# Three matmul passes over split operands in place of f32 matmuls, for the output projection and the memory attention's projections of the last four tiles

## The chip, the cores and the metric

The kernel runs on one core of one Trainium2 chip. The metric is the device time of one execution in microseconds (us), given as the median of several runs. The core has five engines that work side by side, each through its own instruction stream in order: TensorE (PE) multiplies matrices, VectorE (DVE) and ScalarE (ACT) do elementwise work and reductions, GpSimd (POOL) does elementwise work too, and SyncE (SP) issues most of the DMAs. Matmuls read SBUF and write PSUM.

## The reference

One transformer layer over 1024 tokens of width 1024, in f32: a mixer of two sparse attentions, then cross attention to a memory of 256 tokens, then an MLP with a squared ReLU.

```python
x = x + _hybrid_mixer(_rms_norm(x, norm1_g[l]), ...)      # ends with: return o @ w_out
x = x + _memory_xattn(_rms_norm(x, norm2_g[l]), mem, ...)
x = x + _sq_relu_mlp(_rms_norm(x, norm3_g[l]), w_ff_in[l], w_ff_out[l])

def _memory_xattn(h, mem, mem_norm_g, w_xq, w_xk, w_xv, xq_norm_g, xk_norm_g, w_xo):
    q = _rms_norm((h @ w_xq).reshape(B, L, XATTN_HEADS, XATTN_HEAD_DIM), xq_norm_g)
    ...
    p = jax.nn.softmax(s, axis=-1).astype(v.dtype)
    ...
    return o @ w_xo
```

The change bears on three of these products for tokens 512 to 1023: `o @ w_out` (1024 by 1024), `h @ w_xq` (1024 by 512) and `o @ w_xo` (512 by 1024).

## The kernel before

The tokens are eight tiles of 128. The kernel first projects tiles 0 to 3 (`project`, part 0). Then `together` interleaves two generators: the attention of all tiles (`attend`), and a filler, `fill`, that projects the other half, prepares the memory's keys and values, and then runs `between` on tiles 0 and 1, `between` on tiles 2 and 3, `mlp` on tiles 0 to 3, and `between` on tiles 4 and 5. Each step of a generator yields an estimate of its TensorE time, and the filler goes on while its sum is below the attention's sum times a pace (`PACES`). When attention is through, its buffers are given up, the pool `d2` is opened in their place, and `merge` interleaves what is left of the filler with `between` on tiles 6 and 7, in the ratio 70 to 45. Last comes `mlp` on tiles 4 to 7. This order of the program is the priority that a scheduler then uses: it places the instructions of every engine by a simulated timeline, and puts the waits in.

`between` (L894) does, for its `nt` = 2 tiles: load the attention's output `o` from DRAM (eight transfers a tile, L900) and the residual `x`; the product with `w_out` in four chunks of 256 columns, added to `x` by `residual_add` (L891) on VectorE; the second norm (`norm_T2`, L290), which squares the tile into the buffer of the transposed activations and then has TensorE transpose it in groups of four blocks (`to_T`, L268); the product with `w_xq` in two chunks, each followed by attention over the memory (`memory_item`), whose result goes to DRAM (`xo_dr`); this result comes back, is transposed, and is multiplied by `w_xo` in four chunks. There are two streams of it here: tiles 4 and 5 in the pool `dn`, tiles 6 and 7 in the pool `d2`.

`gemm` (L300) is the one function for these products. It takes the activations as a list `xs`. With one entry they are f32: a piece of the weights of 256 rows by 256 columns is fetched by `load_whole` (L261) into a buffer of the rings `whi` and `wlo` by turns, and each block of 128 rows, 128 tokens and 256 columns is one f32 matmul, which appears in the trace as two instructions. With two entries they are a rounded part and a remainder in the type fp32r: `load_w` (L251) fetches the same piece into a buffer of the ring `wraw`, `split_w` (L240) copies it to `whi` (rounded) on one engine and writes the remainder to `wlo` on another, and each block is three matmuls: high by high, high by low, low by high. The engines of `split_w` follow a plan of letter pairs, the first for the copy, the second for the remainder (a: ScalarE, v: VectorE, g: GpSimd): `PLAN_MAIN` is "ag", `PLAN_TAIL` (L46) "ag", "av", "ag" by turns. Before, `between` always calls `gemm` with one entry; `mlp` and the first part of `project` use two. `split_ps` (L234) splits activations: a ScalarE copy and a VectorE subtraction. `to_T` uses it where two outputs are asked for; for one output it copies once, with ScalarE for the first group.

The rings have these depths: in `dn` `wraw` 2, `whi` 4, `wlo` 4; in `d2` `wraw` 3, `whi` 6, `wlo` 6. `xT` (L328) gives the buffers of transposed activations, `xh` and for two entries `xl`; each exists once in a pool, so a second call waits until the first one's readers are done. The MLP at the end uses the same rings and `xh`, `xl` of `d2`.

Of the kernel before, what the change touches and what calls it, by code (L numbers as in the profile page):

```python
# [22 lines left out]
P = 128  # L23
# [22 lines left out]
PLAN_TAIL = ("ag", "av", "ag")  # L46
# [34 lines left out]
REST = 70.0  # L81


def drain(gen):
    for _ in gen:
        pass


def beside(ga, ta, gb, tb):

    da = db = 0.0
    la = lb = True
    while la or lb:
        if la and (not lb or da * tb <= db * ta):
            w = next(ga, None)
            la = w is not None
            da += w or 0.0
        else:
            w = next(gb, None)
            lb = w is not None  # L100
            db += w or 0.0
        if w is not None:
            yield w


def merge(a, b):
    drain(beside(*a, *b))
# [59 lines left out]
def build(nc, tc, I, C, out):  # L167
    v, s, g, te = nc.vector, nc.scalar, nc.gpsimd, nc.tensor
    ctx = ExitStack()
    W = {n: I[n][0] for n in I}  # L170
# [63 lines left out]
    def split_ps(src, hi, lo):  # L234
        s.activation(hi, src, AF.Copy)  # L235
        v.tensor_tensor(lo, src, hi, op=ALU.subtract)  # L236

    plan = {"i": 0, "w": PLAN_MAIN}
# [12 lines left out]
    def load_w(pool, shape, *srcs):  # L251
        raw = ring(pool, "wraw", shape)
        for dst, src in srcs:
            nc.sync.dma_start(dst(raw), src)
        hi, lo = ring(pool, "whi", shape, F32R), ring(pool, "wlo", shape, F32R)
        split_w(raw, hi, lo)
        return hi, lo
# [3 lines left out]
    def load_whole(pool, shape, *srcs):  # L261
        wholes["i"] += 1
        raw = ring(pool, ("whi", "wlo")[wholes["i"] % 2], shape)
        for dst, src in srcs:
            nc.sync.dma_start(dst(raw), src)
        return [raw]
# [33 lines left out]
    def gemm(pool, xs, nk, nt, wsrc, chunks, consume):  # L300

        for ci, parts in enumerate(chunks):
            w = sum(n for _, n in parts)
            gr = []
            for k0 in range(0, nk, KG):
                kn = min(KG, nk - k0)
                srcs, o = [], 0
                for c0, n in parts:
                    srcs.append((lambda r, o=o, n=n: r[:, :, o:o + n],
                                 wsrc[k0 * P:(k0 + kn) * P, c0:c0 + n].rearrange("(k p) n -> p k n", p=P)))  # L310
                    o += n
                ws = load_w(pool, [P, kn, w], *srcs) if len(xs) == 2 else load_whole(pool, [P, kn, w], *srcs)
                gr += [[x[:, k, :] for x in ws] for k in range(kn)]
            for t in range(nt):
                pt = pst(TAGS[pool.name][0], [P, w])
                for k in range(nk):
                    if len(xs) == 1:
                        mm(pt, xs[0](t, k), gr[k][0], k == 0, k == nk - 1)
                        continue
                    wh, wl = gr[k]  # L320
                    xh, xl = xs[0](t, k), xs[1](t, k)
                    mm(pt, xh, wh, k == 0, False)
                    mm(pt, xh, wl, False, False)
                    mm(pt, xl, wh, False, k == nk - 1)
                consume(ci, t, pt)
                yield nk * (5 - len(xs)) * w / 2400.0

    def xT(pool, nt, whole=False):  # L328

        parts = [pool.tile([P, DM // P, nt * P], F32 if whole else F32R, tag="x" + n, name="x" + n)  # L330
                 for n in ("h" if whole else "hl")]
        return (parts, [lambda t, k, x=x: x[:, k, t * P:(t + 1) * P] for x in parts],
                lambda t: [x[:, :, t * P:(t + 1) * P] for x in parts])
# [557 lines left out]
            v.tensor_tensor(dst, pt, dst, op=ALU.add)  # L891
        return add_to

    def between(pool, t0, nt, x2s, keep):  # L894

        o_of = []
        for t in range(nt):
# [6 lines left out]
            nc.sync.dma_start(x2[t], I["x"][0, (t0 + t) * P:(t0 + t + 1) * P, :])  # L904
        add_to = residual_add(x2)
        four = [[(c * 256, 256)] for c in range(4)]
        yield from gemm(pool, [lambda t, k: o_of[t][:, k, :]], 8, nt, W["w_out"], four, add_to)
        _, xf, xt_of = xT(pool, nt, True)

        gb2 = gain2(pool, W["norm2_g"])  # L910
        for t in range(nt):
# [179 lines left out]
    def fill():  # L1091
        for part in range(1, len(PARTS)):
            with tc.tile_pool(name="p2", bufs=1, reuse_waits="tile") as p2:
                yield from project(p2, part, pe, st)
            projected.append(part)
        dn = dn_pool.__enter__()
        yield from memory(dn)
        yield 1, PACES[1]
        yield from between(dn, 0, 2, {}, False)
        yield 3, PACES[2]  # L1100
        x2s = {}
        yield from between(dn, 2, 2, x2s, True)
        yield 3, PACES[3]
        yield from mlp(dn, 0, 4, x2s)
        yield 5, PACES[4]
        yield from between(dn, 4, 2, {}, False)

    rest = fill()
    together(attend(aw, st), rest, projected)
# [4 lines left out]
    d2 = d2_pool.__enter__()  # L1114
    x2s = {}
    rest = (w for w in rest if not isinstance(w, tuple))
    merge((rest, REST), (between(d2, 6, 2, x2s, True), 45.0))
    dn_pool.__exit__(None, None, None)
    drain(mlp(d2, 4, 4, x2s))
    d2_pool.__exit__(None, None, None)  # L1120
# [22 lines left out]
```

## Time and profile before

| | |
|---|---|
| median of 3 runs | 1814.33 us (1814.0 to 1814.47) |
| profiled execution | 1807.76 us |
| its span, first to last instruction | 1806.0 us |
| TensorE busy | 1700.2 us, 94% |
| ScalarE, VectorE, GpSimd busy | 1061.9, 927.8, 887.4 us |
| HBM traffic | 185.38 MB by DMA, 103 GB/s on the mean |
| mean granted TensorE clock | 0.976 |

Rows of the profile name engine, line, operation and buffers as out<-in, with a count and a mean time. Buffers have the names of the kernel's tags: `psD`, `psS`, `psM`, `psPT` are PSUM; `b` holds residuals and the attention's output; `xh`, `xl` are activations, `whi`, `wlo`, `wraw` weights. In stream 4 and 5 the products go to `psD`, in stream 6 and 7 to `psS`. Matmuls are pipelined: a row's mean time is longer than the distance from one start to the next, so rates are taken from starts and counts.

### The profile page before, as it was taken

Reading aid. Unit: us, or ns where it says so; the run is one execution under the profiler, and the core shown is the slowest. Engines: PE = TensorE matmul, PEld = TensorE weight load, DVE = VectorE, ACT = ScalarE, POOL = GpSimd, SP = SyncE. Lnnn points to the kernel's source line nnn. Section 1 sums busy time; section 2 is a strip of 40 time slices with the busy share of each in tenths; the row PEclk is TensorE's granted clock in tenths of the full one; section 3 lists DMA queues with packets and bytes.
Section 4 is the critical chain, followed back from the end, with each engine's and each line's share of the span. In section 5 each row is a group of like instructions: output and inputs, shape, how many; then the busy total and the mean of one; then the engine's idle time right before and its main releaser. Section 6 shows DMA issues by size and latency. Waiting matters only on the chain. (4 is left out here: it accounts for less than half of the span.)

```text
span 1806.0 us, 27690 instructions
## 1 busy us (share of the span) xinstructions
PE 1700.2 (94%) x9134; PEld 1447.8 (80%) x9134; DVE 927.8 (51%) x2343; ACT 1061.9 (59%) x2655; POOL 887.4 (49%) x1015
## 2 busy tenths in 40 slices
PE   5987999899989999999998999999999799999998
PEld 5986888688878777788886888888888687787887
DVE  4545757665874776375754555646524322222221
ACT  4445669797688579855896558994513333333332
POOL 2356647363541355568575667662111144545444
PEclk9998999999999999999999999999999799999999
DMA  6235221366336211212122212226384122222222
GB/s 193 73 121 155 70 68 58 114 196 175 102 109 196 87 59 42 75 65 80 59 75 75 62 65 78 65 74 194 98 284 151 47 87 89 97 91 96 94 95 93
DMA packets 171887, 185.38 MB, mean 103 GB/s; under 512 B 26464, under 2 KB 140896, under 8 KB 171744
## 3 DMA queue, kind: packets, MB, share of 16 engines
q1 hardware_dynamic: 163808, 173.13, 30.3%
q0 software_dynamic: 7936, 10.49, 2.2%
q8 instruction: 72, 1.18, 0.3%
q14 instruction: 71, 0.58, 0.1%
HBM read 162.59 MB, written 20.97 MB: 102 GB/s over the span
## 5 line engine op out<-in xcount | busy, mean ns | idle before, releaser
L249 POOL TENSOR_TENSOR wlo<-wraw,whi 128x512 fp32r<-128x512 f32 (+1 forms) x231 | 310.6, 1351 | 280.9 <-ACT whi L244 252.9
L244 ACT ACTIVATE whi<-wraw 128x512 fp32r<-128x512 f32 (+2 forms) x289 | 181.0, 628 | 250.8 <-PE psS L218 156.8
L218 PE MATMUL psD<-whi,xh 128*128 128x256 f32 (+1 forms) x704 | 191.1, 352 | 4.4 <-ACT whi L244 3.4
L218 PE MATMUL psD<-wlo,xh 128*128 128x256 f32 (+1 forms) x704 | 190.3, 352 | 1.6 <-DMA wlo<-in_w_in_dram 1.0
L236 DVE TENSOR_TENSOR pl<-psPT,ph 128x512 fp32r<-128x512 f32 (+1 forms) x232 | 142.1, 621 | 78.9 <-ACT ph L235 76.3
L218 PE MATMUL psD<-whi,h 128*128 128x512 f32 x512 | 174.3, 403 | 3.7 <-ACT whi L244 1.6
L218 PE MATMUL psS<-whi,h 128*128 128x512 f32 x512 | 162.4, 392 | 5.4 <-DVE b L891 5.4
L680 ACT ACTIVATE S<-S,mn 128x128 f32<-128x128 f32 (+7 forms) x192 | 142.7, 744 | 40.5 <-DVE mn L678 39.0
L685 POOL TENSOR_SCALAR S<-S,sums,gi 128x640 f32<-128x640 f32 (+7 forms) x128 | 107.8, 853 | 114.1 <-DVE sums L683 103.5
L235 ACT ACTIVATE ph<-psPT 128x512 fp32r<-128x512 f32 (+1 forms) x232 | 122.9, 540 | 61.5 <-PE psPT L695 57.1
L249 DVE TENSOR_TENSOR wlo<-wraw,whi 128x512 fp32r<-128x512 f32 (+1 forms) x58 | 56.3, 971 | 170.3 <-ACT whi L244 170.1
L218 PEld LDWEIGHTS psD<-wlo,xh 128*128 128x128 f32 x704 | 132.4, 193 | 13.6 <-DMA wlo<-in_w_in_dram 1.4
L218 PEld LDWEIGHTS psD<-whi,xh 128*128 128x128 f32 x704 | 130.0, 193 | 14.2 <-ACT whi L244 3.8
L695 PE MATMUL psPT<-c_ident,S 128*128 128x128 f32 x816 | 131.8, 277 | 3.9 <-POOL S L685 2.6
L891 DVE TENSOR_TENSOR b<-psS,b 128x512 f32<-128x512 f32 (+1 forms) x80 | 49.9, 636 | 138.5 <-PE psS L218 138.5
L218 PE MATMUL psS<-K,qh 128*128 128x384 f32 (+3 forms) x288 | 112.4, 394 | 8.9 <-DVE mn L678 3.9
L218 PEld LDWEIGHTS psS<-whi,h 128*128 128x128 f32 x512 | 96.0, 188 | 30.4 <-DVE b L891 10.1
L218 PEld LDWEIGHTS psD<-whi,h 128*128 128x128 f32 x512 | 95.5, 189 | 25.8 <-ACT whi L244 2.0
L695 PEld LDWEIGHTS psPT<-c_ident,S 128*128 128x128 f32 x816 | 97.6, 142 | 14.1 <-POOL S L685 4.5
L218 PE MATMUL psD<-wlo,h 128*128 128x512 f32 x256 | 102.6, 404 | 1.1 <-POOL wlo L249 1.1
L218 PE MATMUL psD<-xh,wlo 128*128 128x512 f32 x256 | 101.5, 398 | 0.0
L891 DVE TENSOR_TENSOR b<-psD,b 128x512 f32<-128x512 f32 (+1 forms) x112 | 63.2, 573 | 74.0 <-PE psD L218 66.9
(289 smaller groups left out, 4546.2 us busy)
## 6 DMA issues: line engine op xcount, KB each, us to landing
wraw<-in_w_ff_in_dram SPq DMA_DIRECT2D x128, 256.0 KB, 2.7
wraw<-in_w_ff_out_dram SPq DMA_DIRECT2D x128, 256.0 KB, 2.6
whi<-in_w_out_dram SPq DMA_DIRECT2D x32, 256.0 KB, 3.8
wlo<-in_w_out_dram SPq DMA_DIRECT2D x32, 256.0 KB, 4.3
wraw<-in_w_in_dram SPq DMA_DIRECT2D x24, 256.0 KB, 3.4
q<-st SPq DMA_DIRECT2D x12, 512.0 KB, 2.6
qin<-q SPq DMA_DIRECT2D x44, 128.0 KB, 2.3
x<-in_x_dram SPq DMA_DIRECT2D x8, 512.0 KB, 5.5
```

What stands on the lines that cost most here:

```text
L218: te.matmul(o, a, b, start=start, stop=stop)
L235: s.activation(hi, src, AF.Copy)
L236: v.tensor_tensor(lo, src, hi, op=ALU.subtract)
L244: s.activation(hi, raw, AF.Copy)
L249: (v if l == "v" else g).tensor_tensor(lo, raw, hi, op=ALU.subtract)
L680: s.activation(S, S, AF.Exp, bias=low, scale=-1.0, accum_out=sums[:, hh:hh + 1])
L685: g.tensor_scalar(Ss[hh], Ss[hh], sums[:, hh:hh + 1], 1.0 if gate is None else gate[:, hh:hh + 1], op0=ALU.mult, op1=ALU.mult)
L695: te.transpose(p2[:, j, hh, :], S[:, (c + j) * P:(c + j + 1) * P], ident)
L891: v.tensor_tensor(dst, pt, dst, op=ALU.add)
```

## The change

For tiles 4 to 7, `between` gets `whole=False`. The attention's output is split into a rounded part and a remainder, the transposed activations of `w_xq` and `w_xo` are written as two parts, and the weights of all three products are split as they arrive. `PLAN_TAIL` holds from `between` on tiles 4 and 5 on, where before it began at the opening of `d2`. Tiles 0 to 3 stay as they are.

```diff
-    def between(pool, t0, nt, x2s, keep):
+    def between(pool, t0, nt, x2s, keep, whole):
...
         four = [[(c * 256, 256)] for c in range(4)]
-        yield from gemm(pool, [lambda t, k: o_of[t][:, k, :]], 8, nt, W["w_out"], four, add_to)
-        _, xf, xt_of = xT(pool, nt, True)
+        if whole:
+            xf = [lambda t, k: o_of[t][:, k, :]]
+        else:
+            parts, xf, _ = xT(pool, nt)
+            for t in range(nt):
+                ts_ = slice(t * P, (t + 1) * P)
+                for c in range(0, 8, 4):
+                    split_ps(o_of[t][:, c:c + 4, :], *[x[:, c:c + 4, ts_] for x in parts])
+        yield from gemm(pool, xf, 8, nt, W["w_out"], four, add_to)
+        _, xf, xt_of = xT(pool, nt, whole)
...
-        yield from between(dn, 0, 2, {}, False)
+        yield from between(dn, 0, 2, {}, False, True)
...
-        yield from between(dn, 2, 2, x2s, True)
+        yield from between(dn, 2, 2, x2s, True, True)
...
-        yield from between(dn, 4, 2, {}, False)
+        plan["w"] = PLAN_TAIL
+        yield from between(dn, 4, 2, {}, False, False)
...
-    merge((rest, REST), (between(d2, 6, 2, x2s, True), 45.0))
+    merge((rest, REST), (between(d2, 6, 2, x2s, True, False), 45.0))
```

## The prediction

> **What bounds the kernel now.** I read the page first: its sums and its slices.
>
> ```profile
> span 1806.0 us, 27690 instructions
> PE 1700.2 (94%) x9134; PEld 1447.8 (80%) x9134; DVE 927.8 (51%) x2343; ACT 1061.9 (59%) x2655; POOL 887.4 (49%) x1015
> PE   5987999899989999999998999999999799999998
> ```
>
> TensorE is busy 94% of the span; the slices show two soft places, the beginning and slice 31 (45 us a slice, so about 1400 to 1445 us). The profiled execution took 1807.76 us, its span 1806.0; the median of the runs is 1814.33, 0.4% above. I sum changes against the trace and subtract them from the median.
>
> Next I cut out the stretch that the change touches, by windows. I call the work on tiles 4 and 5 stream A (pool dn) and that on tiles 6 and 7 stream B (pool d2).
>
> ```profile
> core 0: us, PE busy (x) PEld busy (x) DVE busy (x) ACT busy (x) POOL busy (x), PEclk, DMA share, GB/s
> 1060.00:1200.00 140.00, 139.84 (x751) 118.69 (x750) 78.11 (x191) 117.08 (x262) 95.09 (x94) 1.00 0.21 68
> 1234.00:1305.00 71.00, 69.88 (x418) 62.51 (x416) 39.95 (x102) 33.33 (x64) 17.53 (x20) 0.98 0.47 147
> 1305.00:1322.00 17.00, 15.04 (x61) 12.98 (x61) 3.41 (x9) 3.19 (x10) 4.32 (x8) 0.70 0.87 256
> 1322.00:1394.00 72.00, 70.92 (x385) 62.79 (x383) 25.61 (x71) 17.15 (x43) 8.25 (x13) 1.00 0.66 211
> 1394.00:1440.00 46.00, 34.42 (x151) 27.56 (x151) 20.28 (x46) 16.18 (x34) 6.43 (x8) 0.75 0.21 63
> 1400.00:1410.00 10.00, 6.17 (x29) 5.76 (x28) 2.23 (x4) 0.60 (x2) 0.00 (x0) 0.51 0.25 79
> ```
>
> The columns are the stretch, its length, busy time and instructions of TensorE, of its weight loads, VectorE, ScalarE and GpSimd, then TensorE's granted clock, DMA share and GB/s. The reader is to see three kinds of stage. From 1234 to 1305 stream A runs beside the attention of the last tile: TensorE is full (69.88 of 71 us). From 1322 to 1394 B and the rest of A are interleaved: full again (70.92 of 72), the other engines a quarter to a third busy or less. From 1305 to 1322 and from 1394 to 1440 chains of short steps leave it idle, and its clock falls (0.70 and 0.75). So a shorter matmul pays in the first and third stage, and only partly in the others.
>
> Then the ends of the chains, in the timelines of SyncE's DMA queue (SPq) and of TensorE (start, us, what).
>
> ```profile
> 1234.24 0.38 SPq L265 DMA_DIRECT2D whi<-in_w_out_dram  x1
> 1367.05 0.37 SPq L265 DMA_DIRECT2D wlo<-in_w_xo_dram  x1
> 1305.84 8.17 SPq L900 DMA_DIRECT2D b<-o  x16
> 1323.86 1.97 PE L218 MATMUL psS<-whi,b 128*128 128x256 f32 x8 [0.49 <-DMA whi<-in_w_out_dram]
> 1392.58 1.03 PE L218 MATMUL psS<-wlo,xh 128*128 128x256 f32 x4
> 1409.43 1.09 PE L274 MATMUL psPT<-c_ident,relu 128*128 128x128 f32 x4 [3.60 <-DMA relu<-xo]
> 1411.81 1.92 PE L218 MATMUL psS<-whi,xh 128*128 128x256 f32 x4
> 1425.79 1.03 PE L218 MATMUL psS<-wlo,xh 128*128 128x256 f32 x4
> 1439.90 0.78 PE L218 MATMUL psS<-xh,whi 128*128 128x512 f32 x1
> ```
>
> A's weights are fetched from 1234.24 to 1367.05. Attention ends at about 1305; SyncE then issues B's 16 loads of attention output, and B's first `w_out` matmul waits for its weights until 1323.86. B's `w_xq` ends at 1393, its last attention item and a trip through DRAM end at 1409.43, its `w_xo` runs from 1411.81 to 1426.6, and after the norm of four tiles the MLP begins at 1439.90. From there on the kernel is the same in both versions, so the question is when that first MLP matmul starts.
>
> **The change on TensorE.** Which products lie in which stage, by groups of instructions in the four windows; below them two rows of TensorE's timeline, and a window of the head with one of its groups:
>
> ```profile
> L218 PE MATMUL psD<-whi,b 128*128 128x256 f32 x64 | 17.0, 379 | 0.0
> L218 PE MATMUL psD<-whi,xh 128*128 128x256 f32 x16 | 4.1, 379 | 0.0
> L218 PE MATMUL psD<-whi,xh 128*128 128x256 f32 x16 | 5.4, 469 | 0.0
> L218 PE MATMUL psS<-whi,b 128*128 128x256 f32 x64 | 16.8, 382 | 0.9 <-DMA whi<-in_w_out_dram 0.5 <-DVE b L891 0.4
> L218 PE MATMUL psS<-whi,xh 128*128 128x256 f32 x32 | 8.4, 386 | 0.0
> L218 PE MATMUL psD<-whi,xh 128*128 128x256 f32 x32 | 8.3, 382 | 0.0
> L218 PE MATMUL psS<-whi,xh 128*128 128x256 f32 x32 | 9.1, 411 | 0.0
> 1416.29 1.03 PE L218 MATMUL psS<-whi,xh 128*128 128x256 f32 x4
> 1418.02 1.03 PE L218 MATMUL psS<-whi,xh 128*128 128x256 f32 x4
> 80.80:90.80 10.00, 10.00 (x90) 10.00 (x90) 2.05 (x6) 3.08 (x10) 0.99 (x1) 1.00 0.35 105
> L218 PE MATMUL psD<-wlo,xh 128*128 128x256 f32 x30 | 8.2, 276 | 0.0
> ```
>
> Each group has a twin with `wlo`, because whole weights alternate between the two rings, so 64 means 128 instructions. A 128x128x256 product in f32 is two of them. In order: A's `w_out` 64 products and half of `w_xq`, 16 (first stage); the other 16 (second); B's `w_out` 64, B's `w_xq` 32, A's `w_xo` 32 (third); B's `w_xo` 32 (last): 256. In the timeline eight f32 instructions (a row of `whi`, one of `wlo`) start within 1.73 us, so one takes 0.216 and a product 0.432 us. The three-pass price comes from the head, which does the same shapes in three passes with TensorE full: 90 matmuls touch 10 us, and at 276 ns each some 2.5 of them hang over an edge, so 10/87.5 = 0.114 us each and 0.342 a product. Each product saves 0.090 us: 80 in the first stage 7.2, 16 in the second 1.4, 128 in the third 11.5, 32 in the last 2.9, together 23.0 us of TensorE.
>
> **What it adds elsewhere.** The 64 weight loads stay, of the same size, but go through `wraw`. Each now needs a ScalarE copy and a subtraction, by the plan of the tail two in three on GpSimd. The attention output of four tiles is split too (8 copies, 8 subtractions), and 12 transposed groups get a VectorE subtraction.
>
> ```profile
> L244 ACT ACTIVATE whi<-wraw 128x512 fp32r<-128x512 f32 (+2 forms) x289 | 181.0, 628 | 250.8 <-PE psS L218 156.8
> L249 POOL TENSOR_TENSOR wlo<-wraw,whi 128x512 fp32r<-128x512 f32 (+1 forms) x231 | 310.6, 1351 | 280.9 <-ACT whi L244 252.9
> L249 DVE TENSOR_TENSOR wlo<-wraw,whi x58: 609/694/1770, 23.6 to 1780.1; 128x512 fp32r<-128x512 f32 x56, 128x448 fp32r<-128x448 f32 x2
> L236 DVE TENSOR_TENSOR pl<-psPT,ph 128x512 fp32r<-128x512 f32 x59 | 40.3, 687 | 24.6 <-ACT ph L235 23.1 <-PE psD L218 1.4
> ```
>
> ScalarE 72 x 0.63 = 45 us, GpSimd 43 x 1.35 = 58, VectorE (21 + 8 + 12) x 0.69 = 28, over 206 us in which the four windows give ScalarE 70 us, GpSimd 37, VectorE 89. All three stay below 60% busy. That such a mix holds is shown from 1060 to 1200, where the first MLP runs three passes from this same pool beside attention, with ScalarE 117 and GpSimd 95 of 140 us busy and TensorE at 139.84. I take nothing for throughput. VectorE's longest subtraction is 1.08 us over the median; the four that split B's attention output could add 4.3 us, or 0; I take 0, since VectorE idles 46 of 72 us in the third stage. The Trainium skill, "SBUF — State Buffer", section "Who interferes with whom", says that a VectorE instruction with two SBUF inputs and a GpSimd one that reads SBUF shut each other out for a whole instruction; the spread of 694 to 1770 ns agrees with that, and by the rule the time would be up to 1805 us.
>
> **What waits instead.** A whole weight could be fetched 8 (A) or 12 (B) buffers ahead. A split one occupies `wraw` (2 in dn, 3 in d2) until its subtraction is done. The turn of a `wraw` buffer in dn now, from the timelines of SyncE's queue and GpSimd, and the landing of `w_out`'s loads (least, median, most):
>
> ```profile
> 1163.97 7.59 SPq L254 DMA_DIRECT2D wraw<-in_w_ff_in_dram  x4
> 1168.17 1.31 POOL L249 TENSOR_TENSOR wlo<-wraw,whi 128x512 fp32r<-128x512 f32 x1 [1.94 <-ACT whi L244]
> DMA to landing us min/median/max: 2.6/3.9/9.0
> ```
>
> Four loads begin within 7.59 us through two buffers; the first subtraction ends at 1169.48, so a turn is 5.5 us: 2.75 us per weight tile in dn, and with three buffers 1.83 in d2. A's first 24 tiles take 66 us at that pace, as long as the stage. A cannot run ahead there, and its saved TensorE time must go to attention. Bounds: 0 (attention is held by its own chain) and 7.2; I take 4, the middle. In all A has room: 31 tile steps in 133 us, 4.3 each. Behind a split that waits for its DMA stand, on ScalarE, attention's exponentials, on GpSimd the powers of the norms and the `KX`/`VX` loads, on SyncE attention's stores and the `xo` trips; the 1060 to 1200 window has these queues in the same position, the `xo` trip excepted.
>
> Second stage: the first B tile lands when it does now and then needs 0.63 + 1.35 us. TensorE has only `w_xq` before that, so its 1.4 us are lost and 2.0 are added. Bounds -1.4 (A has other work left) and 2.0 + 1.7. The 1.7 stands for the clock: the gap would be 1.4 + 0.49 + 2.0 = 3.9 us, and after the 3.60 us wait at 1409 the clock over 1400 to 1410 was 0.51. I take +2.0.
>
> Third stage: B's `w_out` at ring pace is 16 x 1.83 = 29 us, while TensorE needs 64 x 0.342 = 22 for it; now it ends 30.5 us after its start. A's last attention item and `w_xo` (11 us) fill the difference, since A has its own ring. Split transposes add 4 x 0.69 before B's `w_xq`, beside A's work. Bounds -11.5 (all paid) and -2 (the ring sets B's pace, below); I take -10. Last stage: `w_xo` saves 2.9, two subtractions on the way cost 1.4; its 8 tiles are fetched and split in the idle stretch before (6 buffers), else one turn, 5.5 us, would show. Bounds -2.9 and +4; I take -1.5. The MLP's first raw weights, now behind `w_xo` in the same ring, have the 13 us of the norm as cover.
>
> Sum: -4 + 2 - 10 - 1.5 = -13.5 us, so 1814.3 - 13.5 = 1801 us.
>
> **The rivals.** *All of it is paid*: attention takes the whole 7.2 and filler is always at hand, -23 + 2 = -21 us: 1793. For it, TensorE full in both long stages; against it, the ring pace in the first. *Ring pace instead of TensorE pace*: a weight tile feeds four products, 1.83/4 = 0.46 us each in d2, no better than the 0.432 of f32. If B's chain alone sets the end, `w_out` gains nothing anywhere; only `w_xq` and `w_xo` of B do, 64 x 0.090 = 5.8, less 2.0 and less 1.4 at the transposes: -2 to -3, 1812. Against it, A's 18 us of work in the same stretch. *Slower, by late weights in d2*: landings of `w_out` reach 9.0 us. At a landing of 7 a turn is 9, 3.0 a tile, 48 us for B's `w_out` against 30.5: +17.5, less 4 from the first stage and 5.8, plus 2: about +10, 1824. It decides above a turn of 7.2 us (2.4 a tile). For it, DMA share 0.87 from 1305 to 1322; against it, that burst comes from deep rings, which the small ring cuts off. That the change does not do what it says I can exclude from the head, where the same function makes three-pass matmuls at 0.114 us.
>
> **How the numbers follow.** Forecast (1795 to 1807) 0.42; all paid (1789 to 1795) 0.2; ring pace (1807 to 1816) 0.16; late weights (1816 to 1835) 0.22. A change of 0.2%, 3.6 us, is about what this measurement can tell. Faster: 0.42 + 0.2 + 0.06 of ring pace = 0.68; the same 0.1; slower 0.22. The range drops the best edge and half of the late-weights case: 1790 to 1820.
>
> **What would show it.** In the changed trace: three matmuls of 128x256 at 0.114 us per product in these stages; wraw turns near 5.5 us; TensorE still full in the two long stages, with attention's end 0 to 7 us earlier; the first MLP matmul some 13 us before 1439.9 on the same clock, and the MLP after it unchanged at about 366 us. I am wrong if TensorE waits for `wlo` or `whi` for more than some 5 us in all, or if the first MLP matmul comes later.

## The result, and the profile after

The changed kernel is slower: 1822.1 us median against 1812.09 us for the kernel before on the same chip, a ratio of 1.0049 with a 95% interval of [1.0032, 1.0065], taken over all runs (the two medians alone divide to 1.0055). The forecast was 1801 us, faster. The profiled execution took 1817.73 us. Its page, the sums and the slices:

```profile
span 1816.0 us, 28472 instructions
PE 1692.0 (93%) x9390; PEld 1453.2 (80%) x9390; DVE 963.3 (53%) x2385; ACT 1102.9 (61%) x2727; POOL 942.2 (52%) x1057
PE   5987999799989999999998999998898799999999
```

TensorE's busy sum fell by 8.2 us, and the span grew by 10.0. The windows that the prediction showed of before, now of after (same columns, the last one to the later end):

```profile
1234.00:1305.00 71.00, 62.89 (x465) 57.77 (x466) 52.33 (x113) 43.24 (x81) 31.79 (x31) 0.98 0.41 126
1305.00:1322.00 17.00, 12.82 (x71) 10.80 (x69) 10.31 (x25) 8.48 (x20) 6.79 (x11) 0.75 0.70 212
1322.00:1394.00 72.00, 63.22 (x485) 61.19 (x485) 37.40 (x81) 36.44 (x73) 37.96 (x33) 0.92 0.59 190
1394.00:1453.00 59.00, 45.46 (x256) 39.82 (x256) 27.27 (x59) 22.28 (x44) 15.91 (x16) 0.72 0.37 115
```

In the first stage TensorE had 69.88 us of work before and has 62.89 now: the 7 us are there, and most of them are idle time. In the third stage it had 70.92 of 72 us and now 63.22, at a granted clock of 0.92 instead of 1.00, and the stage lasts longer. The milestones of B follow from the timeline of TensorE (start, us, what); first those of before that the prediction did not show, the last matmul of the first MLP, the end of `w_out` (the last of the four in its row starts at 1354.34) and the starts of the two chunks of `w_xq`:

```profile
1228.28 0.39 PE L218 MATMUL psD<-whi,h 128*128 128x512 f32 x1
...
1353.69 1.03 PE L218 MATMUL psS<-wlo,b 128*128 128x256 f32 x4
...
1358.44 1.08 PE L218 MATMUL psS<-whi,xh 128*128 128x256 f32 x4
...
1386.49 1.08 PE L218 MATMUL psS<-whi,xh 128*128 128x256 f32 x4
```

and those of after:

```profile
1230.75 0.40 PE L218 MATMUL psD<-whi,h 128*128 128x512 f32 x1
...
1323.46 0.80 PE L218 MATMUL psS<-whi,xh 128*128 128x256 f32 x2 [1.07 <-ACT whi L244]
...
1360.03 0.28 PE L218 MATMUL psS<-whi,xl 128*128 128x256 f32 x1
...
1365.12 1.11 PE L274 MATMUL psPT<-c_ident,relu 128*128 128x128 f32 x4 [3.45 <-DVE relu L297]
...
1368.24 0.56 PE L218 MATMUL psS<-whi,xh 128*128 128x256 f32 x1
...
1396.43 0.52 PE L218 MATMUL psS<-whi,xh 128*128 128x256 f32 x1
...
1425.46 0.56 PE L218 MATMUL psS<-whi,xh 128*128 128x256 f32 x1
...
1452.79 0.78 PE L218 MATMUL psS<-xh,whi 128*128 128x512 f32 x1
```

They are, in order, the last matmul of the first MLP, B's first `w_out` matmul, its last one, the first transpose of B's norm (after a wait of 3.45 us), and the first matmuls of the two `w_xq` chunks, of `w_xo` and of the last MLP. From them, and the last store of the attention (1305.15 and 1305.46, shown below):

| step (us) | before | after | difference | forecast |
|---|---|---|---|---|
| to the last matmul of the first MLP | 1228.28 | 1230.75 | +2.5 | |
| from there to the attention's last store | 76.9 | 74.7 | -2.2 | -4 |
| from there to B's first `w_out` matmul | 18.7 | 18.0 | -0.7 | +2 |
| B's `w_out`, first to last matmul | 30.5 | 36.6 | +6.1 | |
| last `w_out` to first `w_xq` matmul | 4.1 | 8.2 | +4.1 | |
| first to second `w_xq` chunk | 28.05 | 28.19 | +0.1 | |
| second `w_xq` chunk to `w_xo` | 25.3 | 29.0 | +3.7 | |
| these four, first `w_out` to first `w_xo` | 87.95 | 102.0 | +14.0 | -10 |
| `w_xo` to the first MLP matmul | 28.1 | 27.3 | -0.8 | -1.5 |
| last MLP | 366.1 | 363.2 | -2.9 | 0 |

The first row is not of the change: the attention's stores lie 2 us later from about 930 us on, and e17 below, which has the program of before up to the last MLP, reaches the same matmul at 1231.05. Counted from that matmul, the last MLP begins 10.4 us later (-2.2 - 0.7 + 14.0 - 0.8), and it is 2.9 us shorter.

The loss is made in the third stage, ten of its fourteen microseconds between B's first `w_out` matmul and its first `w_xq` matmul. TensorE's idle time, from windows cut at these milestones, says how. It grows from 2.5 to 8.4 us ahead of the attention's last store and from 2.4 to 5.2 between that store and B's first `w_out` matmul. In the four steps it grows from 6.5 to 15.4: in `w_out` from 0.4 to 2.0, in the gap after it from 0.0 to 3.9, between the chunks from 0.0 to 2.6, after them from 6.1 to 6.9. So only 1.6 of the 6.1 us of `w_out` are idle time; the rest is mostly work of A that lies there. The groups of TensorE between 1323.46 and 1360.03 hold three rows like this one, 16 products of A's `w_xq`, which before were done ahead of B's first `w_out` matmul:

```profile
L218 PE MATMUL psD<-whi,xh 128*128 128x256 f32 x16 | 4.9, 318 | 1.2 <-ACT whi L244 1.2
```

SyncE's queue shows how B's weights come. Before:

```profile
1305.15 0.59 SPq L709 DMA_DIRECT2D o<-oc  x1
...
1314.99 0.43 SPq L265 DMA_DIRECT2D whi<-in_w_out_dram  x1
...
1317.69 2.12 SPq L265 DMA_DIRECT2D whi<-in_w_out_dram  x1
...
1327.51 0.37 SPq L265 DMA_DIRECT2D wlo<-in_w_out_dram  x1
```

and after:

```profile
1305.46 0.58 SPq L709 DMA_DIRECT2D o<-oc  x1
...
1314.84 1.71 SPq L254 DMA_DIRECT2D wraw<-in_w_out_dram  x3
1316.65 1.03 SPq L254 DMA_DIRECT2D wraw<-in_w_xq_dram  x2
...
1325.82 0.38 SPq L254 DMA_DIRECT2D wraw<-in_w_out_dram  x1
...
1326.84 1.82 SPq L254 DMA_DIRECT2D wraw<-in_w_out_dram  x2
```

Before, five pieces of B's `w_out` were issued from 1314.99 to 1317.69, and the twelfth was issued at 1327.51. After, three are issued, then the ring is full until 1325.82: the first turn of `wraw` takes 11.0 us. The three pieces took 7.9 to 10.3 us to land, about as long as the first ones before (8.7 to 9.0), and the two pieces of `w_xq` behind them, which are A's last, 10.6 and 12.2; before, A's last piece of `w_xq` had been issued at 1285.10. ScalarE's timeline of after says what the first split waited for:

```profile
1322.78 0.63 ACT L244 ACTIVATE whi<-wraw 128x512 fp32r<-128x512 f32 x1 [4.28 <-DMA wraw<-in_w_out_dram]
1324.44 0.63 ACT L244 ACTIVATE whi<-wraw 128x512 fp32r<-128x512 f32 x1 [1.03 <-DMA wraw<-in_w_out_dram]
```

The stretch is the one in which SyncE loads the attention's output and the residuals of tiles 6 and 7. The second effect is on VectorE. The additions of the last `w_out` chunk into the residual, before:

```profile
1351.30 0.42 DVE L891 TENSOR_TENSOR b<-psS,b 128x256 f32<-128x256 f32 x1
...
1355.09 0.42 DVE L891 TENSOR_TENSOR b<-psS,b 128x256 f32<-128x256 f32 x1
```

and after, with one other row of the same timeline:

```profile
1243.98 3.75 DVE L249 TENSOR_TENSOR wlo<-wraw,whi 128x512 fp32r<-128x512 f32 x1 [0.36 <-ACT whi L244]
...
1360.20 0.74 DVE L891 TENSOR_TENSOR b<-psS,b 128x256 f32<-128x256 f32 x2
```

Before, tile 6 was complete 3.8 us ahead of tile 7, and its norm ran under tile 7's matmuls. After, both tiles wait for the same last pieces of weights and are complete within one row (1360.20, x2), so the norm stands in the open. And the subtraction at 1243.98 took 3.75 us, where the median in the prediction was 0.69.

A third effect is the granted clock. The second chunk of `w_xq` ran at a clock of 1.00 before and begins at 0.50 now (first the window of before, then of after, columns as above):

```profile
1386.00:1396.00 10.00, 9.41 (x49) 7.86 (x48) 4.23 (x12) 2.69 (x6) 3.81 (x4) 1.00 0.65 230
```

```profile
1396.00:1402.00 6.00, 6.00 (x29) 6.00 (x29) 0.61 (x1) 0.00 (x0) 0.10 (x1) 0.50 0.80 266
```

In that window the three-pass matmuls start 0.213 us apart, where B's start 0.120 apart at a clock of 1.00. The first 23 of the chunk take 4.8 us in place of 2.6, which is 2.2 of the 3.7 us of the step to `w_xo`. From 1366 to 1372 the clock was 0.53, before 1.00. Both stretches follow idle time of TensorE; no run changes the clock alone.

### The profile page after: what moved, and what is told of

Same layout as the page of the kernel before. It is cut to its first block, busy times and chain, and to the rows that moved or that the text cites. A ratio compares the mean times of both kernels' runs of the same rounds, so it can differ in the third digit from the quotient of the medians.

```text
span 1816.0 us, 28472 instructions
## 1 busy us (share of the span) xinstructions
PE 1692.0 (93%) x9390; PEld 1453.2 (80%) x9390; DVE 963.3 (53%) x2385; ACT 1102.9 (61%) x2727; POOL 942.2 (52%) x1057
## 5 line engine op out<-in xcount | busy, mean ns | idle before, releaser
L249 POOL TENSOR_TENSOR wlo<-wraw,whi 128x512 fp32r<-128x512 f32 (+2 forms) x273 | 366.6, 1350 | 325.3 <-ACT whi L244 318.2
L244 ACT ACTIVATE whi<-wraw 128x512 fp32r<-128x512 f32 x353 | 221.4, 628 | 287.0 <-PE psS L218 142.5
L218 PE MATMUL psD<-whi,xh 128*128 128x256 f32 (+1 forms) x768 | 210.5, 339 | 5.5 <-DVE x L287 3.2
L218 PE MATMUL psD<-wlo,xh 128*128 128x256 f32 (+1 forms) x768 | 210.6, 339 | 4.2 <-DVE wlo L249 2.8
L249 DVE TENSOR_TENSOR wlo<-wraw,whi 128x512 fp32r<-128x512 f32 (+1 forms) x80 | 78.2, 978 | 192.6 <-ACT whi L244 192.2
L218 PEld LDWEIGHTS psD<-wlo,xh 128*128 128x128 f32 x768 | 144.8, 193 | 15.1 <-DVE wlo L249 3.0
L218 PEld LDWEIGHTS psD<-whi,xh 128*128 128x128 f32 x768 | 142.7, 193 | 15.3 <-ACT whi L244 5.6
L218 PE MATMUL psD<-xl,whi 128*128 128x512 f32 x256 | 100.6, 395 | 0.0
```

The source lines that it names most:

```text
L218: te.matmul(o, a, b, start=start, stop=stop)
L244: s.activation(hi, raw, AF.Copy)
L249: (v if l == "v" else g).tensor_tensor(lo, raw, hi, op=ALU.subtract)
```

## The experiments

All ratios are against the kernel before on the same chip, taken over all runs, with a 95% interval. "Stretch" is the time from the last matmul of the first MLP to the first one of the last MLP in the profiled execution; it holds all the work of tiles 4 to 7 up to their MLP. Before it is 211.6 us and the last MLP 366.1; in the changed kernel 222.0 and 363.2. Both columns come from one execution each: e16 and e17, which differ from before only in placement, repeat its stretch to 0.4 us, but e4 and e18, which have the same three-pass work and differ in placement, lie 5.1 us apart, with the profiled execution of e4 3.8 us above the median of its runs and that of e18 4.0 below. A difference of a few microseconds of stretch is therefore weak evidence by itself.

| run | what differs from the changed kernel | ratio | stretch | last MLP |
|---|---|---|---|---|
| e1 | every second piece of weights reused | 0.9980 [0.9969, 0.9991] | 211.6 | 361.3 |
| e2 | d2's rings 6, 9, 9 | 1.0047 [1.0029, 1.0066] | 229.0 | 361.1 |
| e3 | three passes in B alone | 1.0062 [1.0048, 1.0075] | 226.8 | 361.9 |
| e4 | three passes in A alone | 0.9993 [0.9983, 1.0003] | 214.0 | 365.8 |
| e5 | low halves on VectorE | 1.0044 [1.0029, 1.0058] | 223.8 | 362.7 |
| e6 | e2 and e5 together | 1.0004 [0.9993, 1.0016] | 215.4 | 360.9 |
| e7 | order by the price of f32 | 1.0096 [1.0071, 1.0121] | 232.2 | 363.2 |
| e8 | e4 and e5 together | 1.0016 [1.0004, 1.0028] | 214.2 | 365.4 |
| e9 | `w_out` in f32 | 0.9986 [0.9973, 1.0000] | 214.0 | 362.4 |
| e10 | `w_xq`, `w_xo` in f32 | 1.0038 [1.0024, 1.0052] | 222.9 | 362.3 |
| e11 | own buffers for B's split `o` | 1.0043 [1.0025, 1.0062] | 222.2 | 363.3 |
| e12 | e6 and e9 together | 0.9994 [0.9979, 1.0009] | 219.5 | 361.2 |
| e13 | e5, `wraw` of d2 4 deep | 1.0022 [1.0013, 1.0031] | 215.9 | 362.7 |
| e14 | e13 and e11 together | 0.9992 [0.9982, 1.0003] | 214.3 | 362.0 |
| e15 | `w_xq`, `w_xo` of B alone | 0.9998 [0.9988, 1.0009] | 213.2 | 361.8 |
| e16 | before, d2's buffers placed otherwise | 0.9981 [0.9972, 0.9989] | 211.8 | 362.1 |
| e17 | before, `xh` and `xl` placed otherwise | 0.9981 [0.9967, 0.9994] | 212.0 | 362.7 |
| e18 | e4, placed as e16 | 0.9963 [0.9951, 0.9974] | 208.9 | 361.2 |

The theory I began with is that of supply: what B lacks is split weights. Its rival is that the splitting work itself, on ScalarE, VectorE and GpSimd, costs the time. In the expectations S stands for supply, C for the cost of the splitting work or of the changed order of work, E for the engines that split, L for VectorE and GpSimd shutting each other out ("the lock" below), and P for the placement of buffers.

### Is it the supply of weights?

e1_half_load fetches and splits only every second piece of the three projections of tiles 4 to 7 and uses it twice; it leaves out half of these weights' values, and all matmuls remain.

```diff
-                ws = load_w(pool, [P, kn, w], *srcs) if len(xs) == 2 else load_whole(pool, [P, kn, w], *srcs)
+                if len(xs) == 1:
+                    ws = load_whole(pool, [P, kn, w], *srcs)
+                elif pool is p1 or (k0 // KG) % 2 == 0:
+                    ws = load_w(pool, [P, kn, w], *srcs)
```

> Edit: in tiles 4 to 7 only every second piece of w_out, w_xq and w_xo is fetched and split, and used for two pieces' worth of matmuls, so half of the weights' values are left out; every matmul, split activation and store stays. If the supply of split weights (the turn of wraw, with its copy and subtraction) takes the gain (theory S), 32 fewer turns let TensorE run at its own pace: B's w_out takes 22 to 28 us against 36.6 in the changed kernel, attention ends 3 us or more earlier, and the time is 8 to 20 us below the kernel before (ratio 0.989 to 0.996). If the loss is one of order and chains, A being late as filler for B whatever the weights do (theory C), the ratio stays 1.002 to 1.006.

e2_deep_d2 gives the rings of d2 more depth.

```diff
-    "d2": {"b4": 4, "h": 8, "relu": 2, "wraw": 3, "whi": 6, "wlo": 6},
+    "d2": {"b4": 4, "h": 8, "relu": 2, "wraw": 6, "whi": 9, "wlo": 9},
```

> Edit: d2 has wraw 6, whi 9, wlo 9 in place of 3, 6, 6; the split work is the same. If the depth of the ring sets B's pace (theory S, ring), B's w_out takes 26 to 30 us in place of 36.6, and 5 to 8 us come back: ratio 0.999 to 1.002. If the engines that split, or their order, set it (theory E), B's w_out stays at 34 us or more and the ratio at 1.004 to 1.006.

The ratio of e1, 0.9980, lies between what the two theories gave. Its stretch is that of before (211.6 us), and B's `w_out` takes 30.4 us instead of 36.6, but not the 22 that TensorE needs for it. The stretch hides two terms that cancel: the attention's last store comes 72.0 us after the first MLP's last matmul, 4.9 earlier than before, and the four steps from B's first `w_out` to its first `w_xo` matmul still take 92.4 us against 88.0. So about two thirds of the 14.0 us come with the number of weights; the other 4.4 stay. The deep ring did not help, against the expectation; its timelines of VectorE, of GpSimd and its list of waits (total, times, longest) show why:

```profile
1322.76 9.57 DVE L249 TENSOR_TENSOR wlo<-wraw,whi 128x512 fp32r<-128x512 f32 x1 [2.39 <-ACT whi L244]
1332.26 0.41 DVE L985 TENSOR_TENSOR relu<-psD,xsum 128x256 f32<-128x256 f32 x1
```

```profile
1323.13 8.64 POOL L249 TENSOR_TENSOR wlo<-wraw,whi 128x512 fp32r<-128x512 f32 x7
```

```profile
PE psD L218 <- DVE relu L985: 7.2, 1, 7.2
```

With six raw pieces at hand GpSimd ran seven subtractions back to back from 1323.13 to 1331.77. One VectorE subtraction, begun 0.4 us before them, took 9.57 us, and the next VectorE instruction ran only then; TensorE waited 7.2 us for that one. The Trainium skill, "SBUF — State Buffer", section "Who interferes with whom", says that the two engines shut each other out for a whole instruction; this row shows one waiting for the other and more, a VectorE instruction that, though begun first, ends only when a whole run of GpSimd's has ended.

### Is it the two engines, and do both causes hide each other?

e5_all_dve makes all low halves of these weights on VectorE, so that GpSimd has none; e6_all_dve_deep has that and the rings of e2; e8_a_only_dve has it with three passes in A alone.

```diff
-        plan["w"] = PLAN_TAIL
+        plan["w"] = ("av",)
         yield from between(dn, 4, 2, {}, False, False)
...
-    plan["w"] = PLAN_TAIL
     d2 = d2_pool.__enter__()
...
+    plan["w"] = PLAN_TAIL
     drain(mlp(d2, 4, 4, x2s))
```

> Edit: in tiles 4 to 7 every low half of a weight is made on VectorE, none on GpSimd; rings, matmuls and DMAs as in the changed kernel. Theory L (VectorE and GpSimd shut each other out: single subtractions of 3755 ns at 1243.98 in the changed kernel, 9574 ns in the run with deeper rings): the long VectorE instructions of the stage vanish (sum over the usual time from 14 us to under 4), a turn of wraw shortens by 0.6 us, and 4 to 9 us come back: ratio 1.000 to 1.003. If the lock costs nothing on the path (theory S or C): ratio stays at 1.004 to 1.006.

> Edit: as before with all low halves on VectorE, and d2 with wraw 6, whi 9, wlo 9. If the ring of d2 held B's start back and the lock hid that in the run with deeper rings alone: B's w_out takes 26 to 31 us, and the ratio is 0.994 to 0.999, below that of the run with VectorE alone by 0.3% or more. If the ring is no limit: the same ratio as that run.

Neither alone gains (1.0047, 1.0044); together they take nearly all of the loss away (1.0004), and B's `w_out` falls to 30.9 us, with 4 of A's `w_xq` matmuls in it in place of 48. The expectations were missed: e5 lies where the lock would cost nothing, and e6, expected below 0.999, makes up only for the loss. The edit also does more than end the lock: a subtraction takes 0.69 us on VectorE and 1.35 on GpSimd, so pieces are split sooner, and the runs do not separate the two. Neither e5 nor e6 has a subtraction left that takes more than 0.9 us over its usual 0.69. What e5 lost instead is in its timelines of VectorE and ScalarE:

```profile
1362.54 1.37 DVE L249 TENSOR_TENSOR wlo<-wraw,whi 128x512 fp32r<-128x512 f32 x2 [3.52 <-ACT whi L244]
1363.83 0.42 DVE L891 TENSOR_TENSOR b<-psS,b 128x256 f32<-128x256 f32 x1
```

```profile
1361.88 1.31 ACT L244 ACTIVATE whi<-wraw 128x512 fp32r<-128x512 f32 x2 [3.71 <-DMA wraw<-in_w_xq_dram]
1363.09 1.04 ACT L293 ACTIVATE xh<-b 128x1024 fp32r<-128x1024 f32 x1
```

B's last `w_out` matmul starts at 1359.5. The addition of its result stands on VectorE behind two subtractions of `w_xq` pieces, these wait for ScalarE's copies, and those for a DMA (3.71 us). So both norms began 3 to 4 us late, because they were queued behind the splits of weights that the three-deep ring had fetched late. Late weights cost twice: TensorE waits for them, and so does what stands behind their splits.

> Edit: A in three passes with all low halves on VectorE, B in f32. Theory L: A's 3762 ns subtraction at 1245 goes, A is earlier by 2 to 4 us and so is the end: ratio 0.996 to 0.999, against 0.9993 with the mixed plan. If the lock is off the path: 0.999 to 1.001.

In A alone the longer VectorE queue bought nothing: 1.0016 against 0.9993 for e4, slower than either case of the expectation. There the lock is off the path, or its gain is spent on the greater load of VectorE; the runs do not tell these apart.

### Which stream, and which product?

e3_b_only and e4_a_only set `whole` to True for one of the two streams.

```diff
-        yield from between(dn, 4, 2, {}, False, False)
+        yield from between(dn, 4, 2, {}, False, True)
```

> Edit: tiles 4 and 5 (A) keep f32 matmuls, tiles 6 and 7 (B) have three passes. A is then as early as in the kernel before (second half of its w_xq at 1314, not 1324), and B alone pays its ring. Theory S: B's w_out 33 to 37 us with its interleaved work, time 3 to 7 us above before (ratio 1.002 to 1.004). Theory C (A's delay is what costs): ratio 0.996 to 1.000.

```diff
-    merge((rest, REST), (between(d2, 6, 2, x2s, True, False), 45.0))
+    merge((rest, REST), (between(d2, 6, 2, x2s, True, True), 45.0))
```

> Edit: B keeps f32 matmuls, A has three passes. A's weights then come at the pace of two wraw buffers, as in the changed kernel. Theory S: B's w_out is back at 30 us, A's delay of 10 us is filled by B; ratio 0.998 to 1.001. Theory C: A's delay still takes the filler from B, ratio 1.003 to 1.005.

B alone is as slow as both or slower (1.0062), more than either theory gave; its `w_out` takes 40.3 us. A alone makes no difference that the runs show (0.9993). In e4 and e18, where B is f32 and the time is no longer than before, B's `w_out` takes 37.0 and 36.6 us too, with A's work in it and TensorE never idle: the length of that one step is no measure of the loss, only the sum of the four is (90.9 and 88.8 us).

e9_xqxo_only and e10_out_only undo one kind of product in both streams; e15_b_xqxo_only leaves three passes only to `w_xq` and `w_xo` of B; e12_xqxo_dve_deep is e9 with the engines and rings of e6.

```diff
-        if whole:
+        if True:
             xf = [lambda t, k: o_of[t][:, k, :]]
```

> w_out of tiles 4 to 7 goes back to f32 with whole weights; w_xq and w_xo stay in three passes. Theory S (the loss arises in B's w_out: few weights ahead in a three-deep ring, the lock between VectorE and GpSimd, and the wait of the norm for the buffer that w_out's split input uses): from B's first w_out matmul to its first w_xq matmul again about 34.6 us (before 34.6, changed 44.8), first MLP matmul 1437 to 1444 us, ratio 0.998 to 1.002. Theory C (every split product costs, in proportion): half of the loss stays, first MLP matmul about 1446, ratio 1.002 to 1.004.

```diff
-        _, xf, xt_of = xT(pool, nt, whole)
+        _, xf, xt_of = xT(pool, nt, True)
```

> Only w_out of tiles 4 to 7 in three passes; w_xq and w_xo back in f32. Theory S: all of the loss stays, B's first w_out to first w_xq matmul 42 to 47 us, first MLP matmul 1449 to 1455, ratio 1.004 to 1.007. Theory C: half of it, ratio 1.002 to 1.004, first MLP matmul about 1446.

The first matmul of the last MLP in the timelines of e9 and of e10:

```profile
1443.66 0.78 PE L218 MATMUL psS<-xh,whi 128*128 128x512 f32 x1
```

```profile
1454.98 0.78 PE L218 MATMUL psS<-xh,whi 128*128 128x512 f32 x1
```

With `w_out` in f32 the changed kernel's loss is gone (0.9986); with `w_out` alone in three passes the stretch is as long as with all three (222.9 against 222.0). From B's first `w_out` to its first `w_xq` matmul e9 takes 36.5 us and e10 46.5, against 34.6 and 44.8. By these milestones that is the expectation of the supply theory. The ratio of e10, 1.0038, is a little below what that theory gave and lies in the range of the other; seen from the better placement that e10 has too (below), it is 1.0057.

> Only w_xq and w_xo of tiles 6 and 7 in three passes, all of tiles 4 and 5 and all of w_out in f32. Theory S: first MLP matmul 1439 to 1443 us, the MLP after it 361 to 363 us as in every kernel with three passes in d2, ratio 0.996 to 1.000. Theory C (splitting itself costs, and the shorter MLP comes from tiles 4 and 5): ratio 1.000 to 1.002.

> As e9_xqxo_only, with the low halves of the weights made on VectorE and d2's rings 6, 9 and 9 deep, as in e6_all_dve_deep. Theory S (B is held by its chain of short steps; the TensorE time that w_xq and w_xo save is hidden there): B's w_out about 30.5 us, no lock, first MLP matmul 1436 to 1441, ratio 0.996 to 1.000. Theory C (the splitting work itself is the cost): ratio 1.001 to 1.004.

But neither gains on the path: their stretches are 213.2 and 219.5, longer than before, and their ratios of 0.9998 and 0.9994 owe what they have to a shorter MLP. I had expected e12's first MLP matmul at 1436 to 1441 us; it was 1448.9, so the engines and rings that helped `w_out` show no help here. Why its stretch is 5.5 us longer than that of e9 I did not find; the ratios, 0.9994 and 0.9986 with overlapping intervals, hardly show it.

### The order

e7_old_yield has every step of these products report the time of f32, so that the two streams are interleaved as before.

```diff
-                yield nk * (5 - len(xs)) * w / 2400.0
+                yield nk * cost * w / 2400.0
```

> Edit: the products of tiles 4 to 7 report the same cost to the interleaving as f32 matmuls did (4 in place of 3 units), so the order of the program is interleaved as in the kernel before; nothing else. Theory C (the order, which the smaller cost shifts): ratio 0.998 to 1.002. Theories S and L: within 0.15% of the changed kernel, 1.0035 to 1.0065.

It is the slowest (1.0096, stretch 232.2), outside of what any of the theories gave: the new order is no part of the loss, it limits it.

### The norm after w_out

After `w_out` the norm writes `xh`, and in three passes `w_out` itself reads its activations from `xh`. e11_sep_x gives B's split attention output two buffers of its own.

```diff
-            parts, xf, _ = xT(pool, nt)
+            parts, xf, _ = xT(pool, nt, pre="o" if t0 == 6 else "x")
```

> As the changed kernel, but in d2 the split attention output has two buffers of its own, so the norm of tile 6 need not wait for the last w_out matmul of tile 7. Theory S: the gap from B's last w_out matmul to its first w_xq matmul falls from 8.2 us to 4 to 5.5, first MLP matmul about 1449.5, ratio 1.002 to 1.004. Rival (the gap is the lock on VectorE or late w_xq weights): gap 7.5 or more, ratio 1.004 to 1.006.

My expectation failed: the gap stays 8.0 us. The two additions still come together (1361.09 and 1361.42), so while the weights are late the buffer binds nothing. e13_dve_w4 and e14_dve_w4_sep repeat the pair with the low halves on VectorE and one more `wraw` buffer.

> All three projections of tiles 4 to 7 in three passes, low halves of the weights on VectorE as in e5_all_dve, and only wraw of d2 one deeper (4 instead of 3). Theory S: part of what e6_all_dve_deep gained, ratio 1.000 to 1.003, first MLP matmul 1445 to 1451 us, the gap before B's w_xq 7 us or more, since the norm waits for the buffer of w_out's split input. It is the control for e14_dve_w4_sep.

> As e13_dve_w4, and the split attention output of tiles 6 and 7 has two buffers of its own. Theory S (once the weights come early, the norm of tile 6 waits only for the buffer): the gap from B's last w_out matmul to its first w_xq matmul falls to about 4 us, first MLP matmul about 3 us earlier than in e13_dve_w4, ratio 0.998 to 1.001. Rival (both tiles' sums still come together with the last weights): gap and ratio as in e13_dve_w4.

Timelines of VectorE and of ScalarE in e13:

```profile
1358.08 0.42 DVE L891 TENSOR_TENSOR b<-psS,b 128x256 f32<-128x256 f32 x1 [2.29 <-PE psS L218]
...
1361.55 0.41 DVE L891 TENSOR_TENSOR b<-psS,b 128x256 f32<-128x256 f32 x1
```

```profile
1361.33 1.05 ACT L293 ACTIVATE xh<-b 128x1024 fp32r<-128x1024 f32 x1
```

and in e14:

```profile
1357.83 0.42 DVE L891 TENSOR_TENSOR b<-psS,b 128x256 f32<-128x256 f32 x1 [2.06 <-PE psS L218]
...
1362.53 0.42 DVE L891 TENSOR_TENSOR b<-psS,b 128x256 f32<-128x256 f32 x1
```

```profile
1358.29 1.06 ACT L293 ACTIVATE xh<-b 128x1024 fp32r<-128x1024 f32 x1 [3.81 <-DVE b L891]
```

Now the tiles are complete 3.5 and 4.7 us apart again. In e13 tile 6's norm nevertheless starts at 1361.33, right after tile 7's last `w_out` matmul (1361.07), 2.8 us after its own sum is done; in e14 it starts at once. The gap from the last `w_out` to the first `w_xq` matmul falls from 6.1 to 1.7 us and the time from 1.0022 to 0.9992, with intervals that do not meet. So the buffer is a cost of its own, which shows once the weights are in time.

### The shorter last MLP

In every kernel with three passes in d2 the last MLP is some 3 to 5 us shorter, though it is the same program. The groups of its matmuls between 1500 and 1800 us, before, after and in e16 (busy us, mean ns):

```profile
L218 PE MATMUL psS<-whi,h 128*128 128x512 f32 x443 | 140.6, 392 | 4.9 <-DVE b L891 4.9
...
L218 PE MATMUL psS<-xl,whi 128*128 128x512 f32 x204 | 80.3, 394 | 0.0
```

```profile
L218 PE MATMUL psS<-whi,h 128*128 128x512 f32 x414 | 131.4, 392 | 4.5 <-DVE b L891 4.5
...
L218 PE MATMUL psS<-xl,whi 128*128 128x512 f32 x224 | 87.1, 389 | 0.0
```

```profile
L218 PE MATMUL psS<-whi,h 128*128 128x512 f32 x448 | 142.3, 393 | 4.9 <-DVE b L891 4.9
...
L218 PE MATMUL psS<-xl,whi 128*128 128x512 f32 x203 | 79.0, 389 | 0.0
```

Matmuls that involve `xh` or `xl` are 5 ns shorter; those with `h` stay. Their starts lie 231 to 233 ns apart before (medians of some 200 starts each in this window) and 226 to 227 after and in e16. e16_before_layout is the kernel before, with `xh`, `xl` and a `wraw` buffer of d2 claimed ahead of B, so that no work changes, only the place of buffers; e17_before_layout_x claims `xh` and `xl` alone.

```diff
         x2 = [ring(pool, "b4", [P, DM]) for t in range(nt)]
+        if t0 == 6:
+            xT(pool, nt)
+            ring(pool, "wraw", [P, KG, 256])
```

> The kernel before, with xh, xl and one wraw buffer of d2 claimed, and not used, ahead of tiles 6 and 7: only the placement of d2's buffers changes. Theory P (the last MLP is 3 to 5 us shorter in kernels with three passes in d2 because its operands lie elsewhere in SBUF): first MLP matmul about 1440, the MLP 361 to 363 us, its matmuls with xh and xl moving start every 226 us per thousand instead of 231 to 233, ratio 0.997 to 0.9985. Rival (something else of the changed work): MLP 366 us, ratio 0.999 to 1.001.

> As e16_before_layout, but only xh and xl are claimed ahead of tiles 6 and 7, not wraw. If the place of xh and xl decides (the moving operands whose matmuls started 231 to 233 ns apart): the MLP 362 us and ratio 0.997 to 0.999, as in e16_before_layout. If that of wraw, whi or wlo decides: the MLP 366 us and ratio 0.999 to 1.001.

Both give 0.9981 with the stretch of before (211.8 and 212.0 us) and an MLP of 362.1 and 362.7: the order in which the buffers are claimed is worth 0.2%. This is a gift that the changed kernel got beside its change. Against e16 it costs 1.0049 / 0.9981 = 1.0068, 12 us, with 9 to 16 by the two intervals; its profiled stretch is 10.2 us longer than that of e16. By the same division e6 becomes 1.0023, e14 1.0011, e9 1.0005 and e15 1.0017: no kernel with three passes in B is shown to gain by them. e4, with its MLP of 365.8 us, did not get the gift. e18_a_only_layout puts the two that help together: e4's line, and e16's three lines.

> Three passes for tiles 4 and 5 alone, as in e4_a_only, with d2's buffers placed as in e16_before_layout. If the two effects add: 0.9993 x 0.9981 = 0.9974, range 0.996 to 0.9985, the MLP 362 us. If the three passes of tiles 4 and 5 are worth nothing once the placement is right: 0.998, the same as e16_before_layout.

It is the best of all, 0.9963 [0.9951, 0.9974], 6 us below the kernel before. In its profiled execution, the fastest of its eleven runs, the first MLP matmul starts 2 us earlier than before, in TensorE's timeline:

```profile
1437.94 0.78 PE L218 MATMUL psS<-xh,whi 128*128 128x512 f32 x1
```

Three passes for tiles 4 and 5 thus are worth something between nothing and some 0.2%: 0.9993 [0.9983, 1.0003] without the placement, which may be nothing, and 0.9963 / 0.9981 = 0.9982 with it, where the intervals of the two runs just overlap. What e18 gains lies in the first stage: the attention's last store comes 74.1 us after the first MLP's last matmul, in e16 76.8.

## Why the prediction was wrong

**First stage, forecast -4: -2.2.** On the common clock the attention ended 2.2 us earlier, between the bounds of 0 and 7.2, and 4.9 with half of the weights (e1); the middle that was taken had no better reason than the bounds. But TensorE's idle time there grew from 2.5 to 8.4 us, and that was not free: its own filler had filled this stage, and A's weights now came at the pace of two `wraw` buffers. Two of its `w_out` loads were issued early, the other fourteen over 40 us (1237.73 to 1277.77), before all sixteen over 31 (1234.24 to 1264.89). "In all A has room" failed: 16 products of A's `w_xq` slid into B's `w_out`.

**Second stage, forecast +2: -0.7.** The path paid only the copy of 0.63 us, since the first of the three matmuls needs no remainder, and B's first piece landed about 1 us earlier (copy at 1322.78, before the matmul at 1323.86).

**Third stage, forecast -10: +14.** This is the step that failed. It had B's `w_out` at a steady ring pace of 29 us with turns of 5.5 us, and A's work filling the rest; the saved matmul time was to come off the end. Instead TensorE's idle time in the four steps grew by 8.9 us. The first three turns took 11.0 to 12.3 us (the first 1314.84 to 1325.82), the next three 7.9 to 8.5, and only the later ones 4.2 to 6.7, since the first pieces land while B's attention output and residuals are being fetched. Before, twelve pieces were issued within the first 12.5 us; now five were. With A's displaced work `w_out` took 36.6 us. Put at nothing were the norm, which lost 4.1 us with both tiles complete together, and the granted clock in this stage, 1.00 before and 0.92 after, which makes up 2.2 of the 3.7 us before `w_xo`. The prediction priced the clock only in the second stage. That TensorE was 70.92 of 72 us busy said only that A's filler fitted into B's waits. e1 is the test: with half of the weights the four steps lose 4.4 us instead of 14.0, and still none of the forecast gain appears in them.

**Last stage, forecast -1.5: -0.8.** Right in size, but not by its terms. The two subtractions do not stand between the first `w_xo` and the first MLP matmul, where the saving alone should have been 2.9. `w_xo` became 1.1 us shorter from its first matmul to its last: its matmuls start 0.120 us apart in place of 0.114, and the first 20 of them 0.213, at a clock of 0.68 from 1425.46 to 1432.

**The shared port, taken as 0.** The bound of 4.3 us, from the longest row of before, was too small: 9.57 us stood in one row of e2. That the lock by itself costs the changed kernel anything is not shown (e5: 1.0044); a deeper ring alone runs into it (e2), and with both edits nearly all of the loss goes (e6).

**The rivals.** "Late weights in d2" named the place, the cause and the sign, and its +10 us is the size that came (10.0 by the medians). It had a lasting turn of 9 us and 48 us of `w_out`; six turns above its point of 7.2 us came, with A's displaced work, the norm and the clock on top, so that its sum fits is partly luck. The argument against it, that the small ring cuts the burst off, failed: with three pieces under way the landings were as long as before. "Ring pace", at 1812, has the time of e6, but e6 gets there with a last MLP that is 5.2 us shorter; its stretch is 3.8 us longer than before. "All paid" is refuted by e1.

**The MLP after it unchanged.** The program is; its time fell by 2.9 us, as it does when placement alone is changed (e16, e17), and hid a part of the loss.

**What would show it.** At a clock of 1.00 the matmuls were as forecast or nearly: 0.114 to 0.120 us from start to start. TensorE's named waits for `whi` and `wlo` came to 5.9 us (2.8, 1.9 and 1.2), over the 5 I had set; the clearer sign was in ScalarE's wait for `wraw` and in the timeline of the norm.

## What to carry to other kernels

A full engine is the bound only if its work is all on the chain that ends last; if it holds filler, cut the chain out of it and ask of each link what it waits for. A ring of staging buffers has to cover the worst first landing after a burst, not the average turn, and everything queued behind the split on each engine waits with it. Time stages from a mark ahead of the change: here the two executions stood 2.5 us apart before it began. When a change reuses a buffer for a second purpose, ask which step used to start before the first purpose ended; and compare against a kernel with the same placement of buffers before crediting a change with a few microseconds.

## What was unexpected of the hardware

- One VectorE subtraction with both inputs in SBUF took 9.57 us instead of 0.69 while GpSimd ran seven subtractions back to back; shorter cases were 3.75 us.
- Matmuls of 128x128x512 in fp32r that read `xh` or `xl` start every 226 to 227 ns or every 231 to 233 ns, by whether these buffers are claimed early or late in the pool (e17) and nothing else that was changed: 4 us over the last MLP. Which property of the address it is, and whether the places of other buffers matter, was not tried.
- At a granted clock of 1.00, B's three-pass matmuls of 128x256 start 0.120 us apart, those of A and of the head 0.114 to 0.118; whether that too is placement is open. At 0.50 (1396 to 1402) B's start 0.213 us apart.
